# Value products of block 1 moved behind its keys, query products of block 1 into block 0's attention

## The chip, the cores and the metric

The kernel runs on one core of a Trainium2 chip. A core has TensorE (PE, matrix products; PEld is its weight load), VectorE (DVE), ScalarE (ACT) and GpSimd (POOL), which each work through their instructions in program order, and 16 DMA engines that move data between HBM and on-chip memory. SyncE (SP) and GpSimd issue the transfers here. The metric is the device time of one execution in microseconds (us), lower is better.

## The reference

A trunk of two layers over 256 tokens of width 1024, all in float32. Each layer mixes tokens with three groups of attention heads (A, B, C), and then mixes channels with PEER: each token picks, for each of 8 heads, 16 of 16384 one-neuron experts, and gathers the expert's two rows.

```python
for layer in range(DEPTH):
    h = rms_norm(x, attn_norm[layer])
    proj = jnp.einsum('bsd,dp->bsp', h, w_in[layer])        # queries, keys, values of A, B, C
    ...                                                     # norm and rotary on queries and keys
    oa = full_gqa(qa, ka, heads(va))
    ob = dilated_attn(qb, kb, heads(vb))
    oc, _ = banded_attn(qc, kc, heads(vc), LOCAL_HALF_WINDOW, LOCAL_BLOCK, sink_logits[layer])
    mix = concat(_rms(oa), _rms(ob), _rms(oc)) * out_norm[layer]
    x = x + jnp.einsum('bsm,md->bsd', mix, w_out[layer])
    x = x + peer_ffn(rms_norm(x, ffn_norm[layer]), peer_wq[layer], peer_keys[layer], peer_u[layer], peer_v[layer])
# in peer_ffn: per token and head two top-16 over 128 key scores, top-16 of their sums,
#   act = gelu(xc . u[idx]) * gate ;  out = sum over 128 experts of act * v[idx]
```

## The kernel before

**Blocks and stages.** The 256 tokens are two blocks of 128, one token in each partition. For a layer, block 0 goes first: its keys, values and queries are there when the loop `for l in range(L)` comes to the layer (for layer 1 they were made beside layer 0's work). Block 0's attention needs the keys and values of both blocks, so block 1's come first.

**Projections.** `proj_kv(l, b)` makes keys and values in three pieces (`KCH`): piece 0 is 512 columns of keys, piece 1 is 128 columns of keys and 128 of values, piece 2 is 512 columns of values only. Each piece is 8 matrix products over the 1024 inputs into one PSUM bank (tile `pkv`), then ScalarE copies it out (L288 to L295); pieces 0 and 1 then go through norm and rotary on VectorE (`qk_rope`, tiles `kraw`, `kr_`, `ks_`). `keys_t` transposes keys on TensorE (tile `kT`) into `KT` (ScalarE, L306), `queries_t` does it for queries (`qT`, `QT`). `proj_q(l, b)` makes the queries in two chunks of 8 products with 512 columns each (tile `pq`), one yield for each product, and ScalarE copies each chunk out to `qraw` (L321). In the trace a float32 matrix product shows as two instructions and a transpose as one: the 8 products of a piece read x16.

**Block 0's attention.** `attn(l, 0, filler)` writes its order out by hand in `chain_idle`: four groups g of four heads, each with `scores(g)` (tile `sc`), `softmax(g)` (VectorE maxima `m`, ScalarE exponentials L398 into `P`), `divide(g)` (VectorE), `values(g)` (transposes of the weights, tile `pt`, copied by ScalarE L429 into `PT`), `pv(g)` (tile `mix`), then `leave` (VectorE to `mT`, ScalarE squares to `msq`), `norm_sum` (`mss`), `product` and `add` (output projection, tile `wo`, added to `X`). A generator called `filler` is stepped at set places to fill TensorE; before the change it is piece 2 of block 1's projection.

**Routing of the first heads.** After the attention `mixer_in` transposes the normalized block for the expert products, and the lane `rq` runs `route` head by head: products with `wq` (tile `rq`), a copy by ScalarE (L625), key scores (`rs`, copied to `sS`, L636), then some 9 us of VectorE for the three top-16 and the expert numbers (`ei`), and the gate, whose exponential is ScalarE's L698. The loop `while 0 not in DONE` alternates steps of `rq`, of `mixer_in` and of `proj_q(l, 1)`; then the first expert fetch is issued, `rest(pq1)` finishes block 1's queries, and a second head is routed ahead of the gather loop.

**The gather loop.** For each of 256 slots of a layer (2 blocks of 128 experts a token) `fetch` lets GpSimd issue a gather of 1 MB (128 tokens, each with 8 KB of `u` and `v`) into a slab, `dots` (L719, VectorE) forms the products with `u`, `weigh` (L727 to L730, ScalarE) makes a diagonal matrix `dg`, and `gather_up` (L735, TensorE) adds the weighted `v` rows into two PSUM banks `acc`. There are 16 slabs; while the weights of the layer occupy theirs, 8 are left for fetches, so fetch 8 waits until slot 0 was gathered up. All other work of the layer (routing of the other heads, block 1's attention, later the next layer's projections) is recorded between the slots by a planner that counts columns; it fixes the order when the program is built.

**Pools.** Working tiles of 1024 floats share 10 buffers (`big`), PSUM has 6 rotating banks (`ps`) and the two `acc` banks. Nearly all VectorE and TensorE instructions are recorded through a helper, L55, so rows are told apart by their tiles.

Of the kernel before, what the change touches and what calls it, by code (L numbers as in the profile page):

```python
# [59 lines left out]
def tile_trunk(ctx: ExitStack, tc: tile.TileContext, x, wkv, wq_in, w_out, wq, keys, uv0, uv1,  # L60
# [210 lines left out]
    KCH = ((0, 512), (512, 256), (768, 512))  # L271
# [81 lines left out]
    def attn(l, b, filler=None):  # L353
# [20 lines left out]
        def softmax(g):  # L374
            P = PR[g] = big(f"P{l}{b}{g}").rearrange("p (j k) -> p j k", j=4)
            m = sp.tile([128, 4], F32, tag="am", name=f"m{l}{b}{g}")
            nm = sp.tile([128, 4], F32, tag="anm", name=f"nm{l}{b}{g}")
            ls = sp.tile([128, 4], F32, tag="als", name=f"l{l}{b}{g}")
            src = {}
            for i in range(2):  # L380
                kind, _ = pair_info(2 * g + i)
                for s in range(2):
                    j = 2 * i + s
                    sv = SC[g][s][:, i * 256:(i + 1) * 256]
                    if kind == 0:
                        dve.tensor_reduce(out=m[:, j:j + 1], in_=sv, axis=AX.X, op=OP.max)
                        src[j] = sv
                    else:
                        bias = (biasB if kind == 1 else biasC)[:, b, :]
                        dve.tensor_tensor_reduce(out=P[:, j, :], in0=sv, in1=bias, scale=1.0,  # L390
                                                       scalar=NEG, op0=OP.add, op1=OP.max,
                                                       accum_out=m[:, j:j + 1])
                        src[j] = P[:, j, :]
            if g == 3:
                dve.tensor_tensor(out=m, in0=m, in1=SK, op=OP.max)
            dve.tensor_scalar(nm, m, -1.0, None, OP.mult)
            for j in range(4):
                nc.scalar.activation(P[:, j, :], src[j], AF.Exp, bias=nm[:, j:j + 1], scale=1.0,  # L398
                                     accum_out=ls[:, j:j + 1])
            es = None  # L400
            if g == 3:
                es = sp.tile([128, 4], F32, tag="aes", name=f"es{l}{b}")
                dve.tensor_tensor(out=es, in0=SK, in1=nm, op=OP.add)
                nc.scalar.activation(es, es, AF.Exp)
            SM[g] = ls, es

        def divide(g):
            P = PR[g]
            ls, es = SM[g]
            if es is not None:  # L410
                dve.tensor_tensor(out=ls, in0=ls, in1=es, op=OP.add)
            dve.reciprocal(ls, ls)
            if idle:
                dve.tensor_tensor(out=P, in0=P, in1=ls.unsqueeze(2).to_broadcast([128, 4, 256]), op=OP.mult)
            else:
                for j in range(4):
                    nc.scalar.activation(P[:, j, :], P[:, j, :], AF.Copy, scale=ls[:, j:j + 1])  # L417
# [14 lines left out]
        def pv(g):  # L432
            hds = []
            for i in range(2):
                kind, hd = pair_info(2 * g + i)
                hds += [(h % 2, 3 * kind + h // 2, vh, 2 * i + s) for s, (h, vh) in enumerate(hd)]
            lo = [a for a in hds if a[0] == 0]
            hi = [a for a in hds if a[0] == 1]
            for pair in zip(lo, hi):
                for t in range(2):  # L440
                    for o, mt, vh, j in pair:
                        pe.matmul(mix[mt // 4][o * 64:o * 64 + 64, mt % 4, :], V[:, t, vh * 64:(vh + 1) * 64],
                                         PTT[g][:, t, j, :], start=(t == 0), stop=(t == 1),
                                         skip_group_check=True)
# [76 lines left out]
        def chain_idle():  # L521
            scores(0)
            softmax(0)
            scores(1)
            softmax(1)
            divide(0)
            steps(filler, 4)
            rest(keys_t(l, 1, 4, 5))
            rest(filler)
            rest(values(0))  # L530
            scores(2)
            divide(1)
            softmax(2)
            pv(0)
            rest(values(1))
            scores(3)
            divide(2)
            softmax(3)
            pv(1)
            rest(values(2))  # L540
            leave(0)
            divide(3)
            p0 = [product(0, z) for z in range(2)]
            rest(norm_sum(0))
            for z in range(2):
                add(0, z, p0[z])
            pv(2)
            rest(values(3))
            leave(1)
            p1 = [product(1, 0)]  # L550
            rest(norm_sum(1))
            pv(3)
            leave(2)
            p1.append(product(1, 1))
            for z in range(2):
                add(1, z, p1[z])
            rest(norm_sum(2))
            for z in range(2):
                add(2, z, product(2, z))
# [200 lines left out]
    def steps(gen, n):  # L760
        for _ in range(n):
            if next(gen, None) is None:
                return

    def rest(gen):
        for _ in gen:
            pass
# [63 lines left out]
    for l in range(L):  # L831
        if l:
            rest(norm_h(l, 1))
        load(w_out, WO, l, "wo", range(4))
        rest(proj_kv(l, 1, KCH[:2]))
        if l == 0:
            rest(queries_t(0, 0))
        rest(keys_t(l, 1, 0, 4))
        values1 = proj_kv(l, 1, KCH[2:])
        rest(attn(l, 0, values1))  # L840
        load(wq, WQ, l, "wq", range(4))
        open_block(l, 0)
        route_alloc(l, 0)
        rq = Lane(*[route(l, 0, *h) for h in HEADS])

        def routed():
            return sum(len(GATED.get((l, b), ())) for b in range(2))

        hm = mixer_in(l, 0)
        pq1 = proj_q(l, 1)  # L850
        while 0 not in DONE.get((l, 0), ()):
            rq.step()
            steps(hm, 1)
            steps(pq1, 1)
        rest(hm)
        fetch(l, 0, 0)
        rest(pq1)
        finish(rq, until=lambda: routed() > 1)
        bg = Lane(rope_q(l, 1), queries_t(l, 1), attn(l, 1), mixer_in(l, 1))
        dq = pq = 0.0  # L860
        for n in range(256):
            b, s = n // 128, n % 128
            if s == 0:
                ACC[l, b] = [bank(f"acc{z}", f"acc{l}{b}{z}") for z in range(2)]

            dq, pq = min(dq + DVE_SHARE, SAVED), min(pq + PE_SHARE, SAVED)
            while dq > -0.5 and pq > -1.5:
                d, p = dve.spent, pe.spent
                late = routed() < min((n + LEAD) // 16 + 1, 16)
                lanes = (rq, bg) if late or rq.spent < bg.spent else (bg, rq)  # L870
                moved = next((x for x in lanes if (dq if x is rq else pq) > 0 and x.step(n)), None)
                if moved is None:
                    break
                d, p = dve.spent - d, pe.spent - p
                dq, pq = dq - d, pq - p
                moved.spent = max(moved.spent + d + p, max(rq.spent, bg.spent) - 4)
            if (l, 1) not in BEST and not (bg.left or rq.left) or n == 112 and (l, 1) not in BEST:
                finish(bg, rq)
                route_alloc(l, 1)
                open_block(l, 1)  # L880
                rq = Lane(*[route(l, 1, *h) for h in HEADS])
            while routed() < min((n + 3) // 16 + 1, 16):
                if not rq.step():
                    bg.step()
            if n == 132 and l + 1 < L:
                finish(bg)
                load_small(l + 1)
                load(wkv, WKV, l + 1, "wkv", range(5))
                bg = Lane(rope_tables(l + 1), norm_h(l + 1, 0), proj_kv(l + 1, 0), keys_t(l + 1, 0, 0, 4),
                          keys_t(l + 1, 0, 4, 5), once(load, wq_in, WQI, l + 1, "wqi", range(4)),  # L890
                          once(load_late, l + 1), proj_q(l + 1, 0), rope_q(l + 1, 0), queries_t(l + 1, 0))
            if n:
                fetch(l, b, s)
            dots(l, b, s)
            if n == 129:
                settle(l, 0)
            weigh(l, b, s)
            gather_up(l, b, s)
        finish(bg)
        settle(l, 1)  # L900
# [92 lines left out]
```

## Time and profile before

| | |
|---|---|
| device time, median of 3 runs | 1558.68 us (1555.74 to 1562.99) |
| profiled execution | 1560.36 us, of which the span from first to last instruction is 1558.6 us |
| busy in the span | TensorE 1319.9 us (85%), VectorE 1036.2 us (66%), ScalarE 681.5 us (44%), GpSimd 619.3 us (40%) |
| DMA | 578.62 MB, mean 371 GB/s; 536.90 MB of it are the 512 expert fetches |
| first expert fetch issued | at 117.06 us in layer 0, at 892.28 us in layer 1 |

The span has two like halves, one for each layer. In each a stretch without fetches (0 to 117 us, and about 815 to 892 us), which makes keys, values, queries and block 0's attention, is followed by some 700 us of the gather loop. In timeline rows the columns are start, duration, engine, line, operation, output<-inputs, shape and count; in brackets stands how long the engine was idle before, and what ended that.

### The profile page before, as it was taken

To read this page: it belongs to the slowest core of one execution; us is meant where nothing else is said; L and a number is where in the kernel's file an instruction comes from. 1 tells how busy PE (TensorE), PEld (TensorE's weight loads), DVE (VectorE), ACT (ScalarE), POOL (GpSimd) and SP (SyncE) were. 2 spreads that over 40 slices of the span, in tenths; PEclk is the share of its full clock that TensorE was granted. 3 is DMA by queue.
4 is the path that set the end of the run, shared out by engine and by line. 5 is a ranking of instruction groups with operands and counts; after the bars stand their busy time and mean duration, and the time that the engine had idled before them with its cause. 6 is when DMAs were issued, how large, how long until landed. Compare 5 with 4: busy or idle time off the path is not lost. (4 is left out here: it accounts for less than half of the span.)

```text
span 1558.6 us, 15351 instructions
## 1 busy us (share of the span) xinstructions
PE 1319.9 (85%) x3860; PEld 591.2 (38%) x3860; DVE 1036.2 (66%) x3014; ACT 681.5 (44%) x2056; POOL 619.3 (40%) x516
## 2 busy tenths in 40 slices
PE   8896898998868898889878968989998788887777
PEld 4453353443323344433324534444333333332222
DVE  5667868685658777666536587786756767785444
ACT  1323657443434444444323236565434454444333
POOL 0004444555434443423410044545455455555551
PEclk9898999999998999999988989999999999999999
DMA  9308999999999999899991099999999999999996
GB/s 375 156 1 354 420 405 378 395 420 421 419 422 420 421 421 420 343 420 421 422 411 55 17 372 422 414 401 394 421 422 421 422 421 421 422 421 421 422 421 273
DMA packets 81592, 578.62 MB, mean 371 GB/s; under 512 B 9569, under 2 KB 9697, under 8 KB 11873
## 3 DMA queue, kind: packets, MB, share of 16 engines
q0 software_dynamic: 73728, 536.90, 83.6%
q1 hardware_dynamic: 7776, 40.74, 6.5%
q8 instruction: 32, 0.52, 0.1%
q14 instruction: 56, 0.45, 0.1%
HBM read 576.56 MB, written 1.05 MB: 371 GB/s over the span
## 5 line engine op out<-in xcount | busy, mean ns | idle before, releaser
L735 PE MATMUL acc<-uv,dg 128*128 128x512 f32 x2048 | 999.9, 622 | 208.6 <-ACT dg L730 199.5
L714 POOL DMA_INDIRECT uv<-in_uv_dram,ei x512 | 619.1, 1209 | 913.4 <-PE acc L735 309.1
L719 DVE SCALAR_TENSOR_TENSOR uv<-uv,h 128x1024 f32<-128x1024 f32 x512 | 623.8, 1223 | 345.2 <-DMA uv<-in_uv_dram,ei 331.2
L735 PEld LDWEIGHTS acc<-uv,dg 128*128 128x128 f32 x2048 | 367.3, 193 | 768.8 <-ACT dg L730 445.2
L727 ACT ACTIVATE act<-dot 128x1 f32<-128x1 f32 x512 | 102.9, 201 | 542.0 <-DVE uv L719 541.3
L730 ACT ACTIVATE dg<-CI,act 128x128 f32<-128x128 f32 x512 | 205.5, 401 | 16.7
L728 ACT ACTIVATE act<-act,gate 128x1 f32<-128x1 f32 x512 | 150.8, 295 | 16.7
L55 PE MATMUL pkv<-wkv,hT 128*128 128x512 f32 (+1 forms) x192 | 76.0, 545 | 0.7 <-DVE hT L55 0.7
L55 PEld LDWEIGHTS rq<-h2T,wq 128*128 128x128 f32 x512 | 60.8, 192 | 10.6 <-issue 10.0
L55 PE MATMUL wo<-wo,mT 128*128 128x512 f32 x128 | 58.9, 598 | 5.4 <-DVE mT L55 5.4
L55 PE MATMUL rq<-h2T,wq 128*128 128x128 f32 x512 | 61.6, 276 | 0.0
L55 PE MATMUL pq<-wqi,hT 128*128 128x512 f32 x128 | 58.4, 592 | 0.0
L55 DVE MAX8 rv<-sS 128x8 f32<-128x128 f32 x64 | 17.3, 290 | 53.4 <-ACT sS L636 52.9
L55 PEld LDWEIGHTS pkv<-wkv,hT 128*128 128x128 f32 x192 | 37.9, 201 | 37.3 <-issue 34.4
L719 DVE DVE_READ_ACCUMULATOR uv<-uv,h 128x1 f32 x512 | 42.5, 83 | 0.0
L55 PEld LDWEIGHTS wo<-wo,mT 128*128 128x128 f32 x128 | 23.7, 190 | 33.4 <-issue 30.6
L727 ACT ACT_TABLE_LOAD x28 | 35.9, 1283 | 0.5
L55 PEld LDWEIGHTS pq<-wqi,hT 128*128 128x128 f32 x128 | 24.0, 190 | 28.7 <-issue 28.5
L636 ACT ACTIVATE sS<-rs,f_r 128x128 f32<-128x128 f32 (+1 forms) x48 | 16.7, 399 | 41.4 <-PE rs L55 41.4
L55 DVE TENSOR_REDUCE ef<-eq 128x16 f32<-128x512 bf16 x32 | 34.3, 1072 | 0.5
L625 ACT ACTIVATE q<-rq 128x128 f32<-128x128 f32 (+1 forms) x24 | 7.5, 312 | 59.4 <-PE rq L55 59.4
L429 ACT ACTIVATE PT<-pt 128x512 f32<-128x512 f32 x32 | 17.6, 589 | 34.2 <-PE pt L55 34.2
(163 smaller groups left out, 792.4 us busy)
## 6 DMA issues: line engine op xcount, KB each, us to landing
wkv<-in_wkv_dram SPq DMA_DIRECT2D x8, 1024.0 KB, 13.4
wqi<-in_wqi_dram SPq DMA_DIRECT2D x8, 1024.0 KB, 15.2
wo<-in_w_out_dram SPq DMA_DIRECT2D x8, 1024.0 KB, 14.0
wq<-in_wq_dram SPq DMA_DIRECT2D x8, 1024.0 KB, 10.9
uv<-in_uv_dram,ei POOLq DMA_INDIRECT x512, 16.5
wkv<-in_wkv_dram SPq DMA_DIRECT2D x4, 512.0 KB, 6.3
X<-in_x_dram SPq DMA_DIRECT2D x2, 512.0 KB, 6.2
KEYS<-in_keys_dram SPq DMA_DIRECT2D x2, 512.0 KB, 19.7
```

The lines of the kernel that those rows point to most:

```text
L55: return f(*args, **kw)
L429: nc.scalar.activation(PT[:, t, :, :], p.rearrange("p (j q) -> p j q", j=4), AF.Copy)
L625: nc.scalar.activation(q2[:, :n * 128], pq[:, :n * 128], AF.Copy)
L636: nc.scalar.activation(sS[:, p, :n * 128], pk[p][:, :n * 128], AF.Copy, scale=RF[l, b][:, 0:1])
L714: nc.gpsimd.indirect_dma_start(out=t, out_offset=None, in_=uv_rows[l], in_offset=bass.IndirectOffsetOnAxis(ap=EI[l, b, s // 16][:, s % 16: ...
L719: nc.vector.scalar_tensor_tensor(out=t[:, :1024], in0=t[:, :1024], scalar=1.0, in1=H2[l, b], op0=OP.mult, op1=OP.mult, accum_out=DOT[l, b] ...
L727: nc.scalar.activation(a, DOT[l, b][:, s:s + 1], AF.Gelu)
L728: nc.scalar.activation(a, a, AF.Copy, scale=GATE[l, b].rearrange("p h k -> p (h k)")[:, s:s + 1])
L730: nc.scalar.activation(d, ident, AF.Copy, scale=a)
L735: nc.tensor.matmul(ACC[l, b][h], DG[l, b, s], ROW[l, b, s][:, 1024 + h * 512:1536 + h * 512], start=(s == 0), stop=(s == 127), skip_group_ ...
```

## The change

In `proj_kv(l, 1)` all three pieces now run at once: the value products (piece 2) stand directly behind the two key pieces, ahead of the transposes of block 0's queries (layer 0 only) and of block 1's keys. The filler of block 0's attention is no longer piece 2 but `proj_q(l, 1)`, the query products of block 1, of which the first chunk (8 products) is stepped: four products where piece 2 stood, one ahead of `pv(1)`, one ahead of the first output products and two ahead of the second. Only its second chunk is left for the routing stretch after the attention.

```diff
             divide(0)
             steps(filler, 4)
             rest(keys_t(l, 1, 4, 5))
-            rest(filler)
             rest(values(0))
...
             softmax(3)
+            steps(filler, 1)
             pv(1)
             rest(values(2))
             leave(0)
             divide(3)
+            steps(filler, 1)
             p0 = [product(0, z) for z in range(2)]
...
             leave(1)
+            steps(filler, 2)
             p1 = [product(1, 0)]
...
-        rest(proj_kv(l, 1, KCH[:2]))
+        rest(proj_kv(l, 1))
         if l == 0:
             rest(queries_t(0, 0))
         rest(keys_t(l, 1, 0, 4))
-        values1 = proj_kv(l, 1, KCH[2:])
-        rest(attn(l, 0, values1))
+        pq1 = proj_q(l, 1)
+        rest(attn(l, 0, pq1))
...
         hm = mixer_in(l, 0)
-        pq1 = proj_q(l, 1)
         while 0 not in DONE.get((l, 0), ()):
```

TensorE in layer 0, from piece 1 of block 1 (`pkv01512`) to the first scores, before (here a product is one, and digits after a name are layer, block and group or column):

```order
L55 MATMUL pkv01512_414<-wkv0_2_97,hT01_160 128x256 x8
L55 MATMUL qT000_452<-CI_77,qraw00_298 128x128 x4
L55 MATMUL qT004_458<-CI_77,qraw00_298 128x128 x4
L55 MATMUL kT010_464<-CI_77,kraw01_371 128x128 x4
L55 MATMUL sc0000_474<-KT_81,QT_86 128x256
```

The same place in the changed kernel:

```order
L55 MATMUL pkv01512_414<-wkv0_2_97,hT01_160 128x256 x8
L55 MATMUL pkv01768_452<-wkv0_3_103,hT01_160 128x512 x4
L55 MATMUL pkv01768_452<-wkv0_4_105,hT01_160 128x512 x4
L55 MATMUL qT000_462<-CI_77,qraw00_298 128x128 x4
L55 MATMUL qT004_468<-CI_77,qraw00_298 128x128 x4
L55 MATMUL kT010_474<-CI_77,kraw01_371 128x128 x4
L55 MATMUL sc0000_484<-KT_81,QT_86 128x256
```

The 8 value products (`pkv01768`) now stand between piece 1 and the transposes. In layer 1 it is the same without `qT`.

TensorE between the second group of scores and the first transposes of weights (`pt`), before:

```order
L55 MATMUL sc0011_494<-KT_81,QT_86 128x256
L55 MATMUL pkv01768_514<-wkv0_3_103,hT01_160 128x512 x4
L55 MATMUL pkv01768_514<-wkv0_4_105,hT01_160 128x512 x4
L55 MATMUL kT014_523<-CI_77,kraw01_371 128x128
L55 MATMUL pt0000_528<-CI_77,P000_480 128x128 x4
```

In the changed kernel:

```order
L55 MATMUL sc0011_504<-KT_81,QT_86 128x256
L55 MATMUL pq010_525<-wqi0_0_107,hT01_160 128x512 x4
L55 MATMUL kT014_530<-CI_77,kraw01_371 128x128
L55 MATMUL pt0000_534<-CI_77,P000_490 128x128 x4
```

Eight products became four. The other four of the chunk stand one ahead of `mix` of group 1, one ahead of the first `wo`, two ahead of the `wo` of the second head group.

ScalarE from the squares after the attention (`f_sq`) to the copy for head 1's routing (L625), before:

```order
L200 ACTIVATE f00_sq_765,f00_ss_766<-X_75 128x512 x2
L625 ACTIVATE q2000_814<-rq000_796 128x128
L582 ACTIVATE h200_805<-h2p00_0_806,f00_r_773 128x512
L636 ACTIVATE sS000_816<-rs0000_817,f00_r_773 128x128
L636 ACTIVATE sS000_816<-rs0001_818,f00_r_773 128x128
L582 ACTIVATE h200_805<-h2p00_4_822,f00_r_773 128x512
L649 ACTIVATE fx0000_851<-ri000_833 128x256 x2
L321 ACTIVATE qraw01_811<-pq010_812,h01_r_181 128x512
L321 ACTIVATE qraw01_811<-pq011_858,h01_r_181 128x512
L698 ACTIVATE gate00_795<-gate00_795 128x16
L625 ACTIVATE q2001_909<-rq001_900 128x128
```

In the changed kernel (lines after the attention are two higher):

```order
L200 ACTIVATE f00_sq_775,f00_ss_776<-X_75 128x512 x2
L321 ACTIVATE qraw01_524<-pq010_525,h01_r_181 128x512
L627 ACTIVATE q2000_824<-rq000_806 128x128
L584 ACTIVATE h200_815<-h2p00_0_816,f00_r_783 128x512
L638 ACTIVATE sS000_826<-rs0000_827,f00_r_783 128x128
L638 ACTIVATE sS000_826<-rs0001_828,f00_r_783 128x128
L584 ACTIVATE h200_815<-h2p00_4_832,f00_r_783 128x512
L651 ACTIVATE fx0000_861<-ri000_843 128x256 x2
L321 ACTIVATE qraw01_524<-pq011_822,h01_r_181 128x512
L700 ACTIVATE gate00_805<-gate00_805 128x16
L627 ACTIVATE q2001_909<-rq001_900 128x128
```

The copy of the first query chunk moved ahead of head 0's routing; one copy instead of two stands between the expert numbers of head 0 and its gate. VectorE's, GpSimd's and SyncE's instructions stand in the order of before, and so does all of the gather loop.

## Rows read from the trace of the kernel before

**Rows 1.** Busy time by stretch: engines' busy us, clock, DMA share, GB/s.

```profile
138.00:160.00 22.00, 19.69 (x43) 7.39 (x43) 18.88 (x54) 8.98 (x31) 11.25 (x10) 0.94 0.90 355
...
300.00:560.00 260.00, 221.22 (x586) 93.16 (x585) 180.64 (x508) 112.35 (x349) 120.61 (x100) 0.97 1.01 421
...
913.00:936.00 23.00, 20.48 (x46) 7.86 (x45) 19.93 (x54) 9.51 (x32) 11.91 (x10) 0.95 0.89 334
```

**Rows 2.** Timeline of TensorE, layer 0, from block 1's key pieces into the attention.

```profile
41.48 10.49 PE L55 MATMUL pkv<-wkv,hT 128*128 128x512 f32 x32
52.34 1.06 PE L55 MATMUL qT<-CI,qraw 128*128 128x128 f32 x8 [0.38 <-DVE qraw L55]
58.55 1.09 PE L55 MATMUL kT<-CI,kraw 128*128 128x128 f32 x4 [5.15 <-DVE kraw L55]
60.33 3.78 PE L55 MATMUL sc<-KT,QT 64*128 64x256 f32 x16 [0.69 <-ACT KT L306]
64.04 7.87 PE L55 MATMUL pkv<-wkv,hT 128*128 128x512 f32 x16
...
71.86 1.04 PE L55 MATMUL pt<-CI,P 128*128 128x128 f32 x8
72.83 1.13 PE L55 MATMUL sc<-KT,QT 64*128 64x256 f32 x8
```

**Rows 3.** Timeline of VectorE and ScalarE, layer 0: last key rope, first softmax, value copy.

```profile
62.01 0.29 DVE L55 TENSOR_TENSOR kraw<-ks_t,ks_t 128x128 f32<-128x128 f32 x1
62.44 1.42 DVE L55 TENSOR_REDUCE m<-sc 128x1 f32<-128x256 f32 x4
...
66.27 1.22 DVE L55 TENSOR_TENSOR P<-P,l 128x1024 f32<-128x1024 f32 x1
...
72.24 0.68 ACT L295 ACTIVATE V<-pkv,h_r 128x512 f32<-128x512 f32 x1
```

**Rows 4.** Timeline of TensorE, layer 0: idle times later in block 0's attention.

```profile
78.37 1.36 PE L55 MATMUL mix<-PT,V 128*64 128x128 f32 x16 [1.29 <-ACT PT L429]
...
81.80 5.42 PE L55 MATMUL wo<-wo,mT 128*128 128x512 f32 x12 [1.05 <-DVE mT L55]
...
91.49 2.81 PE L55 MATMUL wo<-wo,mT 128*128 128x512 f32 x6 [1.66 <-DVE mT L55]
```

**Rows 5.** Timeline of TensorE and VectorE, layer 1: the same place.

```profile
819.17 10.91 PE L55 MATMUL pkv<-wkv,hT 128*128 128x512 f32 x32
834.50 1.09 PE L55 MATMUL kT<-CI,kraw 128*128 128x128 f32 x4 [4.41 <-DVE kraw L55]
836.27 3.78 PE L55 MATMUL sc<-KT,QT 64*128 64x256 f32 x16 [0.69 <-ACT KT L306]
...
838.38 1.42 DVE L55 TENSOR_REDUCE m<-sc 128x1 f32<-128x256 f32 x4 [0.21 <-PE sc L55]
...
847.25 1.04 PE L55 MATMUL pt<-CI,P 128*128 128x128 f32 x8
```

**Rows 6.** Timeline of TensorE, ScalarE and VectorE, layer 0: routing of the first two heads.

```profile
108.18 13.04 PE L55 MATMUL pq<-wqi,hT 128*128 128x512 f32 x30
...
135.89 3.78 PE L735 MATMUL acc<-uv,dg 128*128 128x512 f32 x4 [9.98 <-ACT dg L730]
...
121.26 0.69 ACT L321 ACTIVATE qraw<-pq,h_r 128x512 f32<-128x512 f32 x1 [6.12 <-PE pq L55]
...
122.08 0.17 DVE L55 TENSOR_REDUCE gs<-gate 128x1 f32<-128x16 f32 x1 [5.86 <-ACT gate L698]
...
124.35 0.55 DVE L55 MAX8 rv<-sS 128x8 f32<-128x128 f32 x2 [1.70 <-ACT sS L636]
...
133.16 1.23 DVE L719 SCALAR_TENSOR_TENSOR uv<-uv,h 128x1024 f32<-128x1024 f32 x1
```

**Rows 7.** Timeline of GpSimd, layer 0: the first and the ninth expert fetch.

```profile
117.06 1.07 POOL L714 DMA_INDIRECT uv<-in_uv_dram,ei  x1 [116.61 <-DVE gate L55]
...
139.94 0.94 POOL L714 DMA_INDIRECT uv<-in_uv_dram,ei  x1 [13.12 <-PE acc L735]
```

## The prediction

> **What bounds the kernel now.** I read the busy times by stretch first. In the long middle of the gather loop the DMA engines are busy without a break and move 421 GB/s [rows 1]; at that rate a fetch of 1.05 MB takes 2.49 us, and TensorE and VectorE have spare time. So in most of the span the time is the fetch stream's, and what can be won is when the stream starts and how often it stops. Two things decide that, once in each layer. First, the chain ahead of the first fetch: keys of block 1, block 0's attention, routing of head 0. Second, a hole right behind the first eight fetches: the rate falls to 355 GB/s in 138 to 160 us and to 334 in 913 to 936 us [rows 1]. The timeline of GpSimd says why: the ninth fetch waits 13.12 us for TensorE's first `acc` products, which free a slab [rows 7]. Those products in turn wait for head 1's routing on VectorE, which ends with the first dots at 133.16 us [rows 6].
>
> **The chain ahead of the first fetch, layer 0.** TensorE ends piece 1 at 41.48 + 10.49 = 51.97 us, does `qT`, waits 5.15 us for the keys' rotary, does `kT`, the scores at 60.33, then the value products for 7.87 us, and only at 71.86 comes to the weights `pt` [rows 2]. Those weights were ready at 66.27 + 1.22 = 67.49 us [rows 3]: 4.37 us are lost to the value products.
>
> After the change the value products run first. In an unbroken stretch an instruction of 512 columns takes 13.04 / 30 = 0.435 us [rows 6], so 16 take 6.95 and end at 58.9. `qT` (1.06) and `kT` (4 at 0.13 = 0.53) follow to 60.5; the rotary had let `kT` start at 58.55, so it no longer limits [rows 2]. ScalarE copies the values (0.68 [rows 3]) from about 59.1, then `QT` and `KT` (about 0.55 each, estimated from the 0.69 us between `kT` and scores [rows 2]), so the scores start near 61.4 instead of 60.33. But they no longer come out of an idle time: 8 instructions took 1.13 us in the unbroken stretch at 72.83, and 3.78 / 2 = 1.89 at 60.33 [rows 2]. The first group is done at 62.5, and the maxima start near 62.75. Before they started at 62.44, because VectorE was busy with the small keys until 62.30 [rows 3]. So they are 0.3 us late. From maxima to finished weights it took 67.49 - 62.44 = 5.05 us, which gives 67.8, with `pt` right behind, at 67.85: **4.0 us** earlier than 71.86. The four query products that now stand there take 8 x 0.435 = 3.48 us behind scores that end at 63.7, so they are done at 67.2 and hide in the wait.
>
> **Layer 1.** Piece 1 ends at 819.17 + 10.91 = 830.08 [rows 5]. Values to 837.0, `kT` to 837.6, value copy and `KT` copy to 838.5, first scores to 839.6, maxima at 839.85: 1.5 us later than 838.38, since there is no `qT` here and the wait for the keys was shorter, 4.41 us [rows 5]. With the same 5.05 us `pt` starts at 844.95 instead of 847.25: **2.3 us** earlier.
>
> **The other four query products.** Each is two instructions, 0.87 us. They stand ahead of TensorE's waits of 1.29, 1.05 and (two of them, 1.74) 1.66 us [rows 4]. What hides them is the work that ends those waits: exponentials on ScalarE, then VectorE's maxima and norm. They cost 0.1 us in each layer; if that cover were gone, 3.5 us. I take 0.1. The query chunk also holds one of six PSUM banks through the attention, so half of the scores of group 3 now waits for VectorE to read group 2; between the two stand `mix` and `pt` (1.36 + 1.04 = 2.4 us [rows 2, 4]) against some 1.42 us of reading [rows 3], so I cost it at nothing, at most at the 1.42.
>
> **Behind the attention.** The `X` sums, transposes and head 0's routing keep their order and move as a whole. ScalarE's copy of the first query chunk (0.69 [rows 6]) now stands ahead of head 0's copies, where ScalarE waits for `rq` anyway: nothing. So the first fetch moves by 4.0 - 0.1 = 3.9 us in layer 0 and 2.2 in layer 1.
>
> Then the hole. TensorE's 30 query instructions lasted 13.04 us [rows 6]; 16 fewer are left, 6.95 us less. ScalarE's last `qraw` copy, at 121.26, held up head 0's gate and so VectorE for 5.86 us, and head 1's products stood behind the same query products [rows 6]. Now head 1's products end 6.95 us earlier against the first fetch; ScalarE has the gate's exponential just ahead of the copy of them, which costs some 0.3. So head 1, the first dots, the first `acc` and the ninth fetch come **6.65 us** earlier against the first fetch. The first eight fetches last 8 x 2.49 = 20 us from about 119 us, so the stream ran dry near 139 and the ninth was issued at 139.94 [rows 7]. At 133.3 it would be in time, and so would those behind it, which are spaced like their gathers. What the hole is worth is the missing rate: (1 - 355/421) x 22 = **3.45 us** in layer 0, (1 - 334/421) x 23 = **4.75 us** in layer 1 [rows 1]. The lower bound is nothing (the hole moves on), the upper is that the whole 6.65 us carry through; I take the missing rate, since the stream can't gain more than it lost.
>
> **Sum.** 3.9 + 3.45 + 2.2 + 4.75 = 14.3 us. The profiled execution took 1560.36 us with a span of 1558.6; that gives 1546.1 and 1544.3. Against the median of 1558.68 it is **1544.4 us**, 0.9% less.
>
> **Rivals.**
> 1. *Only the start counts.* The stream is the bound, and what it makes good behind the eighth fetch it loses again where the other engines limit. Then 3.9 + 2.2 = 6.1 us are left: 1552.6. For it speaks the 421 GB/s over most of the loop, against it that GpSimd waits for TensorE in the hole, not for a transfer [rows 1, 7]. The Trainium skill, Perfetto Trace Analysis, section Identifying the Most-Contended Engine, says that the engine with the highest use is the one to work on, for DMA by bandwidth; by that rule work moved on TensorE would bring no more than this case. The trace agrees with it for the loop, not for the hole.
> 2. *The gaps don't cover.* The change does not fill gaps: each of the four single products pushes what is behind it. 14.3 - 2 x 3.5 = 7.3 us: 1551.4. The waits are as long as the products to 0.1 us, which leaves little room [rows 4].
> 3. *Slower: the value products run at the lower clock.* They stand ahead of every transpose that the scores need, and TensorE runs in order. At the lower clock an instruction of 512 columns took 3.78 / 4 = 0.945 us [rows 6], so 16 take 15.1, 8.2 more, and the first scores 0.76 more: 8.9 us on the chain in each layer. 14.3 - 17.9 = 3.6 us slower: 1562.3. It decides from 7.15 us of delay in a layer, that is from 0.83 us an instruction if the scores are slow too. Against it: the key pieces ahead take 10.49 and 10.91 us without an idle time at the full clock [rows 2, 5], and the value products join them.
> 4. *More than forecast.* The engines' own chain, not the stream, limits behind the hole, and all of 3.9 + 6.65 + 2.2 + 6.65 = 19.4 us come through: 1539.3.
>
> **How the numbers follow.** Forecast 0.70, rival 1 0.13, rival 2 0.07, rival 3 0.06, rival 4 0.04. About 0.5% (7.8 us, 1550.9) is what a measurement of this kernel can tell from no change. Faster by more: the forecast, rival 4 and a few of the runs at the edge of rival 2, 0.76. Rivals 1, most of 2 and half of 3 lie within it: 0.20. Slower: 0.04, the dear end of rival 3. The range goes from rival 4 to just above rival 1, 1539.5 to 1553.
>
> **What would show it.** In the changed trace: no wait ahead of `kT` in layer 0; first `sc` near 61.4 us at 0.14 us an instruction; `pt` near 67.9 and 4 us earlier against the layer's start, in layer 1 2.3 us; idle times ahead of `mix` and `wo` of about 0.4, 0.2 and 0; first fetch near 113.2; VectorE's wait for the gate below 1 us; head 1's MAX8 near 113.8; the ninth fetch near 129.4, before the stream runs dry, and 415 to 421 GB/s in the 20 us behind it. A clock of 0.5 over the value products, a `pt` that comes later than 71.86, or a hole of the old size would make it wrong.

## The result, and the profile after

The changed kernel takes 1541.99 us (median of 6 runs), the kernel before in the same series 1561.16 (6 runs): the ratio is 0.989, with a 95% interval of 0.9856 to 0.9923. The forecast was 1544.4 within 1539.5 to 1553.0. The profiled execution took 1541.82 us with a span of 1540.1, so the span fell by 18.5 us, where the sum said 14.3.

The chain first. The timeline of TensorE, then of VectorE, in layer 0 (start us, us, engine, line, operation, tiles, shape, count, then the idle time before and what ended it) answers to [rows 2, 3, 4]:

```profile
42.44 17.35 PE L55 MATMUL pkv<-wkv,hT 128*128 128x512 f32 x48
...
60.50 0.60 PE L55 MATMUL kT<-CI,kraw 128*128 128x128 f32 x4
62.03 2.00 PE L55 MATMUL sc<-KT,QT 64*128 64x256 f32 x16 [0.93 <-ACT KT L306]
63.96 3.70 PE L55 MATMUL pq<-wqi,hT 128*128 128x512 f32 x8
...
68.39 1.06 PE L55 MATMUL pt<-CI,P 128*128 128x128 f32 x8 [0.63 <-DVE P L55]
...
72.50 1.13 PE L55 MATMUL sc<-KT,QT 64*128 64x256 f32 x8
...
74.92 1.35 PE L55 MATMUL mix<-PT,V 128*64 128x128 f32 x16 [0.23 <-ACT PT L429]
...
78.36 5.42 PE L55 MATMUL wo<-wo,mT 128*128 128x512 f32 x12 [0.19 <-DVE mT L55]
...
87.95 2.84 PE L55 MATMUL wo<-wo,mT 128*128 128x512 f32 x6
...
62.96 0.29 DVE L55 TENSOR_TENSOR kraw<-ks_t,ks_t 128x128 f32<-128x128 f32 x1
63.20 1.42 DVE L55 TENSOR_REDUCE m<-sc 128x1 f32<-128x256 f32 x4
```

All 48 key and value instructions run in one stretch; `kT` no longer waits. The 16 scores take 2.00 us instead of 3.78: before they came shortly behind an idle time of 5.15 us and ran at the lower of TensorE's two clock levels (granted clock 0.50 in 60.3 to 64.1 us, and the same in layer 1 in 836.2 to 840.1), now at the upper one (1.00 in 60 to 100 and in 826 to 870 us). `pt` waits for the weights `P` by 0.63 us where it used to be 4.37 us late, and the waits ahead of `mix` and the two `wo` are 0.23, 0.19 and none, where they were 1.29, 1.05 and 1.66. Against the start of the key pieces `pt` came 30.38 us later before, and 25.95 us later now.

The same place in layer 1, TensorE and VectorE, against [rows 5]:

```profile
808.78 17.45 PE L55 MATMUL pkv<-wkv,hT 128*128 128x512 f32 x48
...
827.50 2.00 PE L55 MATMUL sc<-KT,QT 64*128 64x256 f32 x16 [0.83 <-ACT KT L306]
...
833.87 1.06 PE L55 MATMUL pt<-CI,P 128*128 128x128 f32 x8 [0.63 <-DVE P L55]
...
828.66 1.42 DVE L55 TENSOR_REDUCE m<-sc 128x1 f32<-128x256 f32 x4 [1.22 <-PE sc L55]
```

Then the routing of the first two heads, on TensorE, VectorE and GpSimd, against [rows 6, 7]:

```profile
104.67 6.17 PE L55 MATMUL pq<-wqi,hT 128*128 128x512 f32 x14
...
125.88 3.58 PE L737 MATMUL acc<-uv,dg 128*128 128x512 f32 x4 [10.24 <-ACT dg L732]
...
112.97 0.17 DVE L55 TENSOR_REDUCE gs<-gate 128x1 f32<-128x16 f32 x1 [0.28 <-ACT gate L700]
...
114.08 0.55 DVE L55 MAX8 rv<-sS 128x8 f32<-128x128 f32 x2 [0.53 <-ACT sS L638]
...
113.53 1.07 POOL L716 DMA_INDIRECT uv<-in_uv_dram,ei  x1 [113.08 <-DVE gs L55]
...
129.74 0.94 POOL L716 DMA_INDIRECT uv<-in_uv_dram,ei  x1 [6.45 <-PE acc L737]
```

Fourteen query instructions stand there instead of thirty, VectorE waits 0.28 us for head 0's gate instead of 5.86, and the ninth fetch comes 16.21 us behind the first, where it came 22.88 behind. The stretches behind the eighth fetch (us, busy time of each engine, granted clock, DMA share, GB/s), against [rows 1]:

```profile
134.00:156.00 22.00, 20.05 (x56) 8.66 (x58) 19.14 (x50) 11.09 (x35) 13.52 (x11) 1.00 1.01 422
892.00:915.00 23.00, 21.30 (x45) 8.15 (x44) 19.85 (x54) 8.89 (x31) 11.51 (x10) 0.89 1.01 422
```

Both holes are gone: 422 GB/s where there were 355 and 334, as much as in the long middle of the loop. (In layer 1 the stretch shown starts 13 us behind the first fetch, the one of before 21 us behind it; 21 us behind it, in 899.6 to 922.6 us, the changed kernel moves 421.)

Where the 18.5 us went, from the fetch times of both traces:

| stretch | before, us | after, us | change | forecast |
|---|---|---|---|---|
| start to block 1's key pieces | 41.48 | 42.44 | +0.96 | 0 |
| key pieces to first fetch, layer 0 | 75.58 | 71.09 | -4.49 | -3.9 |
| first to 33rd fetch, layer 0 (the hole) | 81.10 | 77.12 | -3.98 | -3.45 |
| 49th to 57th fetch, layer 0 | 25.94 | 22.97 | -2.97 | 0 |
| rest of layer 0 | | | +0.13 | 0 |
| first `hTp` to first fetch, layer 1 | 75.00 | 71.92 | -3.08 | -2.2 |
| first to 33rd fetch, layer 1 (the hole) | 81.12 | 76.51 | -4.61 | -4.75 |
| rest of layer 1 | | | -0.46 | 0 |

Four rows carry the gain as forecast, 16.2 us of the 18.5; the fifth, 2.97 us at the 49th fetch, was in no step. A second trace of each kernel (shown further below) has the four rows, layer 1 counted from its key pieces, at -4.51, -4.57, -3.67 and -5.87, 18.6 us together, in a span that is 15.6 us shorter; so a single row is good to 1 us or so.

### The profile page after: what moved, and what is told of

Same layout as the page of the kernel before. It is cut to its first block, busy times and chain, and to the rows that moved or that the text cites. A ratio compares the mean times of both kernels' runs of the same rounds, so it can differ in the third digit from the quotient of the medians.

```text
span 1540.1 us, 15349 instructions
## 1 busy us (share of the span) xinstructions
PE 1312.9 (85%) x3860; PEld 584.8 (38%) x3860; DVE 1036.2 (67%) x3014; ACT 681.6 (44%) x2056; POOL 620.5 (40%) x516
## 3 DMA queue, kind: packets, MB, share of 16 engines
HBM read 576.56 MB, written 1.05 MB: 375 GB/s over the span
## 6 DMA issues: line engine op xcount, KB each, us to landing
wqi<-in_wqi_dram SPq DMA_DIRECT2D x8, 1024.0 KB, 15.5
```

## The experiments

Each ratio is against runs of the kernel before on the same chip; where two ratios are compared, both intervals count. The fetch times are of one trace each; that of e1 is of the longest of its twelve executions (1565.6 us, median 1556.4). Block 1 has sixteen query products of two instructions; the change moves eight of them, and where an expectation says "all eight" of products behind the attention it means these beside the other eight. The third column counts the query instructions that stand ahead of head 1's products or of the first `acc`.

| kernel | ratio, 95% interval | `pq` left | key pieces to first fetch, layer 0 / 1 | first to ninth fetch, layer 0 / 1 | first to 33rd, layer 0 / 1 |
|---|---|---|---|---|---|
| before | 1 | 32 | 75.58 / 73.11 | 22.88 / 23.05 | 81.10 / 81.12 |
| changed | 0.989 (0.9856 to 0.9923) | 16 | 71.09 / 70.07 | 16.21 / 16.38 | 77.12 / 76.51 |
| e1_values_only | 0.9971 (0.9955 to 0.9987) | 32 | 72.22 / 71.52 | 23.36 / 24.14 | 81.38 / 83.05 |
| e2_queries_only | 0.9987 (0.9969 to 1.0004) | 24 | 75.36 / 71.81 | 21.60 / 21.77 | 78.69 / 80.16 |
| e5_slot_only | 0.9924 (0.9894 to 0.9954) | 24 | 71.08 / 70.05 | 19.56 / 19.61 | 76.70 / 78.63 |
| e10_queries_twice | 0.9952 (0.9933 to 0.997) | 32 | 71.13 / 70.09 | 22.90 / 23.05 | 82.23 / 81.24 |
| e6_no_gaps | 0.9926 (0.9902 to 0.995) | 16 | 73.70 / 72.67 | 16.42 / 16.02 | 77.46 / 76.90 |
| e7_values_twice | 0.9976 (0.9962 to 0.9991) | 16 | 77.99 / 76.96 | 16.41 / 16.37 | 76.66 / 76.24 |

### The two halves

The values' half:

```diff
-        pq1 = proj_q(l, 1)
-        rest(attn(l, 0, pq1))
+        rest(attn(l, 0, iter(())))
...
+        pq1 = proj_q(l, 1)
         while 0 not in DONE.get((l, 0), ()):
```

> Half of the change alone: block 1's value products stand behind its keys, but all eight query products stand behind block 0's attention, as in the kernel before; none of them is stepped inside the attention. My theory (start and hole are two separate gains): from the start of block 1's key pieces to the first fetch about 71.1 us in layer 0 (after 71.09, before 75.58), the layer-1 chain about 3.1 us shorter than before, but first to ninth fetch as before, 22.9 us, with the hole behind the eighth fetch of the old size. Time 5.5 to 8 us under the kernel before, about 1554. Rival 1 (only the start counts) expects the whole gain of the change already here: 17 to 19 us under the kernel before, about 1542.

It gained 4.5 us (0.29% of 1560), less than the 5.5 to 8 expected, with the ninth fetch no earlier than before against the first (0.5 and 1.1 us later). Rival 1's 17 to 19 us are far off. But the chain is 1.1 and 1.5 us longer than the changed kernel's, which my theory did not have. The timeline of TensorE in layer 0 shows why, and the stretch around it gives the clock:

```profile
67.96 1.16 PE L55 MATMUL pt<-CI,P 128*128 128x128 f32 x8 [4.12 <-DVE P L55]
69.05 2.08 PE L55 MATMUL sc<-KT,QT 64*128 64x256 f32 x8
71.06 1.64 PE L55 MATMUL mix<-PT,V 128*64 128x128 f32 x16
```

```profile
66.00:72.00 6.00, 4.04 (x26) 2.99 (x28) 3.65 (x9) 3.52 (x13) 0.00 (x0) 0.73 0.00 0
```

With nothing between the scores and `pt`, TensorE idles for 4.12 us, the granted clock is 0.73 in this stretch, and the eight scores behind it take 2.08 us instead of 1.13. In layer 1 it is the same (4.11 us idle, 2.08 us for the scores). The four query products in that place do more than use a wait: with them alone (e5 below) the clock is 1.00 in 60 to 100 us, and the chain is as short as the changed kernel's.

The queries' half leaves the values where they were:

```diff
-            rest(filler)
+            rest(vals)
...
+            steps(filler, 1)
             pv(1)
...
+            steps(filler, 1)
             p0 = [product(0, z) for z in range(2)]
...
+            steps(filler, 2)
             p1 = [product(1, 0)]
```

> The other half alone: the value products stay where the kernel before has them, and four of the eight query products stand in the three gaps of block 0's attention; the other four stay behind it. My theory: pt and first fetch as before (75.6 us from the start of the key pieces in layer 0), first to ninth fetch shorter by 4 x 0.87 = 3.5 us, so about 19.4 instead of 22.9; the eight fetches last some 20 us, so the hole nearly goes: 3 to 4 us in layer 0, 3 to 5 in layer 1, time 6 to 9 us under the kernel before, about 1553. Rival 1 (only the start counts): no difference, within 1 us of the kernel before. Rival 2 (gaps don't cover): first fetch 3.5 us later in each layer, time about as before.

2.0 us, with an interval that reaches to no difference: a miss. The ninth fetch came 1.3 us earlier instead of 3.5. TensorE did its part (22 instructions instead of 30 in that stretch, and head 1's maxima came 3.4 us earlier against the first fetch in both layers), but VectorE stopped in head 1's routing. Its timeline there, layer 1:

```profile
892.61 0.55 DVE L55 MAX8 rv<-sS 128x8 f32<-128x128 f32 x2 [1.69 <-ACT sS L639]
897.19 0.17 DVE L55 TENSOR_SCALAR ia<-rpos 128x16 int32<-128x16 int32 x1 [0.35 <-DVE rpos L55]
899.28 0.17 DVE L55 TENSOR_SCALAR ib<-ib 128x16 int32<-128x16 int32 x1 [1.78 <-remote]
```

In layer 0 five pauses of 0.27 to 0.53 us stand at these instructions and just behind them. From these maxima to the sum of head 1's gate it is 10.4 to 10.5 us in both layers here and 8.3 to 8.7 in all the other kernels. The profile names no instruction of this core that ended the long pause (`remote`). GpSimd issues the last two of the eight fetches in that stretch (896.05 and 897.29 us), but in the changed kernel the same instructions run beside such issues without a pause; the cause stays open. What the half does settle is that the two halves together (6.5 us) are not the change (17 us by the ratio), even with the 2.1 us a layer that the pauses took: the slot behind the scores is only free once the values are gone, so four of the eight products belong to neither half.

### The hole by itself

```diff
-            for k in range(8):
+            for k in list(range(8)) * (1 + b * c):
                 pe.matmul(p, HT[l, b][:, k, :], w_qi(l, k, c),
```

> The changed kernel with its attention as it is, but the eight query products that are left behind the attention are computed twice (the second time over the first, same result): sixteen instructions, 6.95 us of TensorE, put back ahead of head 1. This makes the hole of the kernel before again and touches nothing else. My theory: first fetch as in the changed kernel (71.1 us from the start of the key pieces), first to ninth fetch 16.2 + 6.7 = 22.9 us, the rate behind the eighth fetch down to 330 to 360 GB/s, and by the 33rd fetch 4.0 us lost in layer 0 and 4.6 in layer 1: 8.6 us slower than the changed kernel, about 1550.6. Rival 1 (only the start counts): as the changed kernel, 1542. Rival 4 (the whole shift counts): 13.4 us slower, 1555.4.

This is the run that decides on rival 1. The start is untouched (71.13 and 70.09 us), the hole is back, and the kernel is slower than the changed one by 0.0062 of 1560 = 9.7 us by the ratios, whose intervals do not overlap. TensorE, GpSimd and the stretch behind the eighth fetch:

```profile
104.09 13.04 PE L55 MATMUL pq<-wqi,hT 128*128 128x512 f32 x30
```

```profile
135.86 0.93 POOL L716 DMA_INDIRECT uv<-in_uv_dram,ei  x1 [13.15 <-PE acc L737]
```

```profile
134.00:156.00 22.00, 20.25 (x44) 7.61 (x44) 18.95 (x52) 9.09 (x31) 11.94 (x10) 0.92 0.90 338
```

By the 33rd fetch 5.1 us are lost in layer 0 and 4.7 in layer 1, of 6.69 and 6.67 us by which the ninth fetch is later: less than rival 4's whole shift, and in layer 0 more than the 3.45 of the missing rate. The rest of each layer adds 3.1 and 1.4 us in this trace, where the 49th to 57th fetch alone take 2.9 us more in each layer, a stop described with the second traces. So against rival 4 stands the 33rd fetch alone: the times are too loose to tell 8.6 from 13.4 us.

### The gaps

Both runs leave out the three `steps(filler, …)` lines of the gaps; the second also has all eight in the slot:

```diff
-            steps(filler, 4)
+            steps(filler, 8)
```

> The changed kernel without the query products in the three gaps: only the four in the place of the value products stay inside block 0's attention, twelve of the sixteen stand behind it. My theory after the first experiments (the four in that place fill a wait of 4.12 us, and with them the clock stays at 1.00; the gap products only serve the hole): start of the key pieces to first fetch as in the changed kernel, 71.1 us, no clock below 1.00 between 60 and 100 us; first to ninth fetch 16.2 + 3.5 = 19.7 us; half of the hole is back: 2 us a layer, 3 to 5 us slower than the changed kernel, about 1546. Rival 4 (the whole shift of head 1 counts): 7 us slower than the changed kernel. Rival 1 (only the start counts): as the changed kernel.

> The changed kernel with all eight moved query products in the place of the value products and none in the gaps. My theory (the gaps cover the four products): the eight take 6.96 us there, the wait they fill is 4.1 us, so pt and the first fetch come 2.8 us later in each layer (73.9 instead of 71.1 us from the start of the key pieces); first to ninth fetch as in the changed kernel, 16.2; time 5 to 6 us above the changed kernel, about 1547.5. Rival 2 (the gaps don't cover, each gap product pushes what is behind it): the 3.5 us are only paid at another place, first fetch and time as in the changed kernel, about 1542.

The first answers rival 2: the chain without products in the gaps is 71.08 us long, with them 71.09; they cost nothing. Its time is 5.3 us above the changed kernel's by the ratios, but their intervals overlap, so only the trace tells what the gap products bring. There the rate behind the eighth fetch is 416 GB/s in layer 0, so 19.56 us from first to ninth fetch are already short enough, and the 33rd fetch is late only in layer 1 (2.1 us): less than the 2 us a layer that were expected. What it loses beyond that lies in stops further on in the loop, as between the 33rd and the 57th fetch of layer 0 (3.1 us).

In the second, TensorE in layer 0:

```profile
64.10 7.13 PE L55 MATMUL pq<-wqi,hT 128*128 128x512 f32 x16
71.08 0.27 PE L55 MATMUL kT<-CI,kraw 128*128 128x128 f32 x1
71.18 1.04 PE L55 MATMUL pt<-CI,P 128*128 128x128 f32 x8
```

The eight overrun the wait: `pt` has no idle time ahead of it, and the first fetch is 2.6 us later in both layers (forecast 2.8), 5.2 us together; the time is 5.6 us above the changed kernel's by the ratios, again with overlapping intervals. The same four products cost 2.6 us in the slot and nothing in the gaps.

### A delay on the values' place

```diff
-            for k in range(8):
+            for k in list(range(8)) * (1 + b * (c0 > 512)):
                 pe.matmul(p[:, :n], HT[l, b][:, k, :], w_kv(l, k, c0, n), …)
```

> The changed kernel with block 1's value products computed twice at their new place (the second time over the first, same result): 6.95 us of TensorE more ahead of every transpose that the scores need. It prices a delay on that part of the chain, which rival 3 rests on. My theory: the delay is on the path from end to end, first fetch 6.9 us later in each layer, loop as in the changed kernel, time 13.8 us above it, about 1556. If the chain had cover there (VectorE's rotary of the small keys, the copy of the keys), it would be 5 us or less in a layer.

The first fetch is 6.90 and 6.89 us later against the key pieces, and the time 13.4 us above the changed kernel by the ratios. There is no cover at this place: what the value products take longer, the first fetch comes later, and the time agrees. That is rival 3's price. Its condition did not come: the clock of the changed kernel was 1.00 in 42 to 100 us, and in 808.8 to 826 us of layer 1.

### The query products behind head 1

Four runs tried to take the hole away without the attention, or to go further than the change. Two put the remaining query products behind head 1's routing, in the kernel before and in the changed one:

```diff
-            steps(pq1, 1)
...
-        rest(pq1)
         finish(rq, until=lambda: routed() > 1)
+        rest(pq1)
```

> The hole taken away in another way, with block 0's attention untouched: the kernel before, but all eight query products of block 1 are put behind head 1's routing instead of ahead of it. My theory: first fetch as before, since head 0 doesn't wait for them; ninth fetch at least 6.7 us earlier against the first (16.2 us or less instead of 22.9), no hole behind the eighth fetch, time 8 to 12 us under the kernel before, about 1551. Rival 1 (only the start counts): no difference. Rival 4 (the whole shift of head 1 carries through): 13 us or more under the kernel before.

> The changed kernel, with the four query products that are left behind the attention put behind head 1's routing as well. My theory (the stream is the bound once it does not run dry): head 1 and the ninth fetch come some 3 us earlier against the first fetch (13 instead of 16.2 us), first fetch as after, and the time is 0 to 2 us under the changed kernel, since no hole is left that this could fill. Rival 4 (the engines' own chain limits behind the hole): 3 us in each layer, 6 us under the changed kernel.

In the kernel before this brought nothing (ratio 1.0009, 0.9994 to 1.0024), and first to ninth fetch took 23.62 us; only the first fetch itself came 0.8 us earlier against the key pieces (74.76), as no query product stood in head 0's routing any more. TensorE and GpSimd in layer 0:

```profile
116.77 15.46 PE L55 MATMUL pq<-wqi,hT 128*128 128x512 f32 x32
...
136.36 3.38 PE L735 MATMUL acc<-uv,dg 128*128 128x512 f32 x4 [2.36 <-ACT dg L730]
```

```profile
125.63 0.94 POOL L714 DMA_INDIRECT uv<-in_uv_dram,ei  x1 [2.49 <-PE pq L55]
...
140.02 0.94 POOL L714 DMA_INDIRECT uv<-in_uv_dram,ei  x1 [6.58 <-PE acc L735]
```

I had overlooked two things. The products still stand ahead of the first `acc`, with 15.46 us of TensorE and their copies on ScalarE ahead of `dg`. And their weights `wqi` lie in the same sixteen slabs (`N8`, `slab`) as the fetched rows: the sixth to eighth fetch now wait for `pq` to let go of them. In the changed kernel the same edit was neutral too: 0.9877 (0.9858 to 0.9896), first to ninth fetch 17.05 us and not 13, since the ninth was issued at 129.28 us, with the first `acc` still behind the query products.

The other two took the products into the gather loop as background work:

```diff
-            steps(pq1, 1)
...
-        rest(pq1)
...
-        bg = Lane(rope_q(l, 1), …)
+        bg = Lane(pq1, rope_q(l, 1), …)
```

> The kernel before with nothing moved in the attention, but with all sixteen query products of block 1 run as background work inside the gather loop, so that they stand neither ahead of head 1's routing nor ahead of the first accumulation. In the experiment that only reordered them against head 1's routing they stayed ahead of the first accumulation (15.46 us of TensorE) and the ninth fetch didn't move. My theory (the hole is a gain of its own): first fetch as before, first to ninth fetch 14 to 15.5 us instead of 22.9, no hole behind the eighth fetch, 4 us in layer 0 and 4.6 in layer 1, time 6 to 10 us under the kernel before, about 1552. Rival 1 (only the start counts): within 1.5 us of the kernel before. Rival 4 (the whole shift counts): 14 us or more.

> The changed kernel, with the eight query products left behind the attention taken out of the way altogether: they run as background work inside the gather loop, behind the first accumulations. My theory (the stream no longer runs dry, so head 1 can't win more): first to ninth fetch 14 to 15.5 us instead of 16.2, bounded by VectorE's routing of head 1, and the time within 2 us of the changed kernel. Rival 4 (the engines' own chain limits): as much faster as the ninth fetch is earlier, 1 to 2 us in each layer, and more if the loop's other stops go.

The kernel before with this: 1.0006 (0.9986 to 1.0025), a miss. GpSimd's timeline:

```profile
119.97 0.94 POOL L714 DMA_INDIRECT uv<-in_uv_dram,ei  x1 [0.30 <-issue]
132.10 0.94 POOL L714 DMA_INDIRECT uv<-in_uv_dram,ei  x1 [11.19 <-PE acc L735]
```

Only four fetches are issued ahead of the first `acc`, not eight, because all four slabs of `wqi` are still in use; the hole moves forward to the fifth fetch and the ninth comes at 26.18 us, although the first `acc` starts 11.94 us behind the first fetch instead of 18.83. In the changed kernel with it, where half of `wqi` is done inside the attention, six are issued ahead of the first `acc`. So early fetches, query products and head 1 hang together by the slabs: moving the products later trades one wait for another, moving them earlier, as the change does, frees both. The changed kernel's ratio with it is 0.9881 (0.9853 to 0.9909), the same time; that the ninth fetch came at 19.88 us and not at 14 to 15.5 was a miss, and with the background work in another order the fetches can't be compared one by one.

None of these versions beats the changed kernel by more than the intervals.

### The 2.97 us at the 49th fetch

Both kernels unaltered, profiled once more.

> The changed kernel unaltered, for a second trace. The question is the 2.97 us that the first trace of it gains between the 49th and the 57th fetch against five other kernels with the same work there. My theory (TensorE's clock falls at another moment, by chance): the second trace has the low clock either over the 12 accumulations ahead of the gap or over the 8 behind it; only in the latter it loses the 3 us. A rival (the change itself moves that stretch): the second trace is there like the first.

> The kernel before unaltered, for a second trace. By my theory (chance) the 8 accumulations that took 6.67 us at the clock of 0.50 behind a gap of 3.45 us may this time run at 1.00 in 3.7 us, and the stop of 3 us may be missing or stand elsewhere; by the rival (it belongs to the order before) it is there again. First to ninth fetch 22.9 us in both cases.

TensorE in that stretch, first the changed kernel's two traces, then the two of before:

```profile
240.58 7.11 PE L737 MATMUL acc<-uv,dg 128*128 128x512 f32 x12 [2.40 <-ACT dg L732]
...
250.01 3.70 PE L737 MATMUL acc<-uv,dg 128*128 128x512 f32 x8 [1.75 <-ACT dg L732]
```

```profile
194.85 2.51 PE L737 MATMUL acc<-uv,dg 128*128 128x512 f32 x4 [2.83 <-ACT dg L732]
...
241.58 5.42 PE L737 MATMUL acc<-uv,dg 128*128 128x512 f32 x12 [2.41 <-ACT dg L732]
...
251.00 5.27 PE L737 MATMUL acc<-uv,dg 128*128 128x512 f32 x8 [3.44 <-ACT dg L732]
```

```profile
248.10 5.42 PE L735 MATMUL acc<-uv,dg 128*128 128x512 f32 x12 [2.41 <-ACT dg L730]
...
257.53 6.67 PE L735 MATMUL acc<-uv,dg 128*128 128x512 f32 x8 [3.45 <-ACT dg L730]
```

```profile
247.89 5.42 PE L735 MATMUL acc<-uv,dg 128*128 128x512 f32 x12 [2.40 <-ACT dg L730]
...
257.32 6.68 PE L735 MATMUL acc<-uv,dg 128*128 128x512 f32 x8 [3.45 <-ACT dg L730]
```

The work is the same in all four. Where the twelve accumulations run slowly (7.11 us, clock 0.76 in 240.5 to 247.5), the eight behind the next idle time run in 3.70 and nothing is lost; where the twelve are fast, TensorE idles longer behind them (3.45 us instead of 1.75), and the eight take 5.27 to 6.68 (clock 0.53 in 257.4 to 264.0 of before). The 49th to 57th fetch of layer 0 take 22.97 us in the changed kernel's first trace, 24.54 in its second, which also loses 1.68 us a little earlier, and 25.94 in both of before. So the cheap placement does not come with the change as such: the changed kernel has it in one trace and not in the other. Layer 1 says the same of the kernel before: there the same eight fetches take 22.97 us in its first trace and 25.81 in its second. The changed kernel's second trace has a span of 1545.3 us, that of before one of 1560.9: 15.6 us. What stays open is whether the hole makes the dear placement likelier. The cheap one, 22.97, stands in three of the traces without a hole (changed, e6, e7) and not in e4 or the second one of the changed kernel, and in none of the six with a full or nearly full hole (before twice, e1, e2, e3, e10). In layer 1 two of those six have it (before once, e3), so the hole does not exclude it; that is too few to say more.

## Why the prediction was right

- **Values ahead of the scores.** Right in mechanism, 0.6 and 0.9 us too small (4.49 for 3.9, 3.08 for 2.2). The scores started 19.59 us behind the key pieces (forecast 19.9) and ran at 0.125 us an instruction (0.14). In layer 0 the scores limit nothing, though: the maxima start when VectorE is done with the small keys, 20.96 us behind the key pieces before and 20.76 now, where the sum had them 0.3 us later than before. In layer 1 the key pieces of before had lost 0.3 us to the lower clock (10.91 us, granted clock 0.80 in 819.2 to 821; 10.59 in its second trace), which the prediction read as full clock. The sixteen value instructions took 17.45 - 10.59 = 6.86 us (forecast 6.95), the scores started 18.72 us behind the key pieces (19.3), the maxima began 19.88 us behind the key pieces, 0.67 later than before and not 1.5, and `pt` followed 5.21 us behind them (5.05).
- **Four products in the slot.** They hide, as forecast, with 0.63 us to spare. That the clock depends on them (e1) was not in the working; it made no difference to the sum, since the change has both parts. That it held is luck in this respect: without them the chain would have been 1.1 and 1.5 us longer.
- **Four products in the gaps.** Forecast 0.1 us a layer; e5 against the changed kernel shows 0.0. Rival 2 is out. The fear of the query chunk's PSUM bank is answered by the changed trace (e5 holds the bank too): the eight scores of group 3 run in 1.13 us at 72.50, with no idle time.
- **Head 1's shift.** 6.67 us against the first fetch, forecast 6.65. MAX8 was forecast at 113.8 and came at 114.08, the ninth fetch at 129.4 and came at 129.74. That these absolute times fit so well is in part luck: a start 0.96 us later and a chain 0.6 us shorter than forecast nearly cancel.
- **The hole.** 3.98 and 4.61 us where the missing rate gave 3.45 and 4.75; put back by itself (e10) it cost 5.1 and 4.7. In the second pair of traces it is 4.6 and 5.9. The step "since the stream can't gain more than it lost" gives the size to 1 us or a little more; it is too strict as a bound, as e10 lost 1.7 us more than that in layer 0. The Trainium skill's rule that stood with rival 1 (Perfetto Trace Analysis, Identifying the Most-Contended Engine) would have left these 8 to 10 us out; its next section, Optimization Strategy, which says to look for the gaps on the engine that binds and for the semaphore that ends them, agrees with this trace: the gap in the stream of fetches was ended by `acc` on TensorE [rows 7], and TensorE work was what to move.
- **The sum.** 14.3 us forecast, 18.5 in the first pair of traces: 1.5 us of mis-sized chain, 0.4 of mis-sized holes, 2.97 of the clock's placement, -0.96 from a later start in the load stage, 0.3 in the rests. Without the clock's 2.97 it is 15.5. So part of the distance between 1544.4 and 1541.99 is this placement, which I could not have read from one trace of before. By the ratio the change is worth 17 us, with 12 to 22 within its interval, so the times do not tell the forecast's 14.3 from what was measured; that the terms are too small rests on the traces.
- **Rival 3** had the right price (e7: each us there puts the first fetch off by one), and its condition did not come.

My first account of why it works, two gains that add, was too simple: e1 and e2 together give 6.5 of 17 us, and e3 and e9, which should have removed the hole from the other side, left it there (23.62 and 26.18 us to the ninth fetch) and gave nothing.

## What to carry to other kernels

Work that an in-order engine does "meanwhile" has to be followed to everything it holds: here moving query products off the stretch ahead of the first accumulation freed the gate, the next head and the weight slabs that the fetches need. Moving them later freed the next head as well (in e3 its gate's sum came 9.2 us behind the first fetch instead of 15.6), but kept the slabs, and in e3 the first accumulation, waiting. To judge a hole, put it back by itself with doubled work (e10) rather than removing half of a change, since halves may need each other. A filled wait can be worth more than the work in it, if the engine's clock is low behind the empty one (1.1 and 1.5 us here, e1 against e5).

## What was not expected of the hardware

- TensorE's clock was 0.73 over 66 to 72 us where it had idled for 4.12 us between scores and `pt` (e1), and 1.00 where 3.70 us of products stood in that wait (the changed kernel).
- The same instructions of the same kernel got the low clock at another place from one execution to the next: 7.11 us for twelve accumulations and then 3.70 for eight in one trace, 5.42 and 5.27 in the other. The eight fetches that follow differ by 1.6 us between these two, and by 2.8 between the two traces of the kernel before in layer 1 (22.97 and 25.81).
- VectorE stopped 1.8 to 2.1 us in the middle of head 1's routing in one kernel (e2), in both layers, between small instructions that follow from each other (8.3 to 8.7 us from maxima to gate elsewhere, 10.4 to 10.5 here). No run explains it.
